# Two PSUM banks in the attention: one per kind of product, or both for every kind in turn

## The chip, the cores and the metric

The kernel runs on one core of one Trainium2 chip. The metric is the time of one execution on the device in microseconds (us). Matrix products run on TensorE (PE in the profile; its weight loads are PEld), elementwise work on VectorE (DVE), ScalarE (ACT) and GpSimd (POOL), and DMAs are issued by SyncE (SP).

## The reference

One block over 1024 tokens of width 1024: a normalized input is projected, an mLSTM branch and a differential attention branch are computed from the projections, both are gated, mixed, projected out and added to the input. The change lies in the attention branch (8 heads, values of width 128, two maps of queries and keys of width 64 in each head):

```python
def diff_attention(q, k, v, lam):
    ...
    def one_block(qb):
        scores = jnp.einsum('bqhjd,bkhjd->bhjqk', qb, k) * scale
        p = jax.nn.softmax(scores, axis=-1)
        p_diff = p[:, :, 0] - lam * p[:, :, 1]
        return jnp.einsum('bhqk,bkhd->bqhd', p_diff, v)
    ...
att = rmsnorm(att, da_subln_g[layer]) * (1.0 - lambda_init)
y_b = att.reshape(B, S, DA_WIDTH).astype(x.dtype) * jax.nn.silu(b_z)
```

## The kernel before, in words

The kernel has stages that follow each other on TensorE: the projections of the mLSTM branch, then the attention, then the mLSTM, then the products behind both branches. Every float32 matrix is split into a high and a low part, so a product is three matmuls.

In the attention a head has eight blocks of 128 queries. For block t of head h these units are recorded:

- S(h,t), `scores` (L924): 12 matmuls into two PSUM tiles of two banks each. VectorE takes the maximum of each (L927), ScalarE the exponential of each (L929), and VectorE joins both maps into one (L935).
- T(h,t,0) and T(h,t,1), `transposes` (L131 in the helper `tr`): four transpositions each into a bank with the tag T. ScalarE casts them to the high part pH (L948), then VectorE subtracts to get the low part pL (L949). Only then is the bank free.
- PV(h,t2,0) and PV(h,t2,1), `pv` (L960): the products with v for two blocks, 24 matmuls into one bank with the tag PV, which ScalarE copies to att (L962).
- M(h,t2), `squares` (L131): two transpositions of att into a bank with the tag PV, which ScalarE squares and sums in place (L972).
- G(h,0) and G(h,1), `scale` (L131): four transpositions into a bank T, read by VectorE (L992).

PSUM has eight banks: four for S, one T, one PV, and two (tag pj) for the projections that are woven in as filler. The filler is the projections of the next head (q and k with the rotary embedding in `da_proj`, v in `da_v`, z) and gate projections; L429 and L451 are their matmuls. Rotated q and k are cast and split (L863 to L869), written to memory by SP as stk (L873) and read back in another layout as qq and kst (L875) before the scores of the next head use them.

The order on TensorE is written by a planner, `Weaver`. It keeps a clock in its own units: each unit has a cost, the units it comes after, and, for a bank, a time `hold` for which the bank stays taken once the unit is done. At every step it takes the list (attention or filler) whose first unit is ready earliest:

```python
        if u.tag:
            held = sorted(self.free.get(u.tag, []))
            n = self.banks.get(u.tag, 1)
            if len(held) >= n:
                t = max(t, held[-n])
```

So a tag that is not named in `banks` counts as one bank. The planner's counts are its own; how many banks a tag really has is set by `banks("ps1", ...)`, and a real bank is handed out in rotation. TensorE keeps the planned order; the order on the other engines is set by the framework's scheduler from the recorded program.

## Time and profile before

| | |
|---|---|
| median of 3 runs | 1750.76 us (1749.43 to 1751.54) |
| profiled execution | 1750.27 us |
| its span | 1748.5 us |
| mean granted TensorE clock | 0.992 |
| attention with its filler | about 440 to 1155 us of the span |

The profile is of one execution. A busy TensorE row is pipelined, so matmuls overlap in it. In the rows of the prediction a group stands as line, engine, operation, output tile <- input tiles; in rows in order of time the first number is the start and the second the duration, both in us, and a bracket at the end gives idle time of that engine before the instruction and who ended it.

### The profile page before, as it was taken

The page shows a single profiled execution, that of the slowest core. Times are in us where ns is not written, and L with a number is a line of the kernel's source. Part 1 is how long each engine was busy: PE and PEld are TensorE (multiplying, and loading weights), DVE is VectorE, ACT ScalarE, POOL GpSimd, SP SyncE. Part 2 cuts the span into 40 slices and gives each one's busy share as a digit, 9 for nine tenths or more (in the row PEclk, how much of TensorE's full clock was granted, in tenths as well). Part 3 has the DMA queues.
Part 4 walks back from the last instruction along what each step waited for, and adds up shares of the span by engine and source line. Part 5 has one row for each costly group of instructions (what it writes and reads, how often), then busy time and mean ns, then how long its engine had stood idle before and what let it go on. Part 6 is the DMA issues. An engine that isn't in the chain of part 4 may idle for free. (4 is left out here: it accounts for less than half of the span.)

```text
span 1748.5 us, 25290 instructions
## 1 busy us (share of the span) xinstructions
PE 1664.4 (95%) x9431; PEld 1390.5 (80%) x9431; DVE 990.8 (57%) x1799; ACT 780.6 (45%) x1554; POOL 608.6 (35%) x680
## 2 busy tenths in 40 slices
PE   7999999999999999999999989999999989999998
PEld 5777887877877877787778767789999877888887
DVE  5777678772476665666656655414666753226533
ACT  7454555552354544454445444424555643112211
POOL 4767666664142323323341322132312311222000
PEclk9999999999999999999999999999999999999999
DMA  5343434434241214230422041146545327444222
GB/s 179 92 136 110 145 109 133 138 116 150 79 128 62 89 37 133 73 91 24 139 75 82 27 130 61 43 146 192 149 143 150 105 77 255 145 126 150 85 85 84
DMA packets 182540, 195.55 MB, mean 112 GB/s; under 512 B 10905, under 2 KB 134130, under 8 KB 182418
## 3 DMA queue, kind: packets, MB, share of 16 engines
q1 hardware_dynamic: 181506, 192.35, 35.4%
q8 instruction: 74, 1.21, 0.3%
q10 hardware_dynamic: 912, 1.59, 0.2%
q14 instruction: 48, 0.39, 0.1%
HBM read 130.89 MB, written 63.01 MB: 111 GB/s over the span
## 5 line engine op out<-in xcount | busy, mean ns | idle before, releaser
L429 PE MATMUL pj<-hH,wH 128*128 128x512 f32 x640 | 267.3, 418 | 3.8 <-DVE hl L864 1.9
L429 PE MATMUL pj<-hH,wL 128*128 128x512 f32 x640 | 252.3, 394 | 1.8 <-POOL wL L207 1.8
L429 PE MATMUL pj<-hL,wH 128*128 128x512 f32 x640 | 251.4, 393 | 0.2 <-DVE hL L580 0.2
L209 POOL TENSOR_TENSOR wL<-raw,wH 128x1024 fp32r<-128x1024 f32 x41 | 99.5, 2426 | 273.2 <-ACT wH L204 264.9
L929 ACT ACTIVATE e<-S,nm 128x1024 f32<-128x1024 f32 x128 | 142.6, 1115 | 106.6 <-DVE nm L927 106.3
L949 DVE TENSOR_TENSOR pL<-T,pH 128x512 fp32r<-128x512 f32 x128 | 88.2, 689 | 136.7 <-ACT pH L948 136.6
L927 DVE TENSOR_REDUCE nm<-S 128x1 f32<-128x1024 f32 x128 | 150.6, 1218 | 25.5 <-PE S L924 24.8
L429 PEld LDWEIGHTS pj<-hH,wH 128*128 128x128 f32 x640 | 121.0, 189 | 40.4 <-issue 17.2
L451 PE MATMUL pj<-wH,hH 128*128 128x256 f32 x512 | 150.2, 293 | 0.8 <-DVE zg L882 0.5
L451 PE MATMUL pj<-wL,hH 128*128 128x256 f32 x512 | 144.9, 283 | 1.4 <-POOL wL L207 1.4
L429 PEld LDWEIGHTS pj<-hH,wL 128*128 128x128 f32 x640 | 120.9, 189 | 30.4 <-POOL wL L207 3.2
L451 PE MATMUL pj<-wH,hL 128*128 128x256 f32 x512 | 144.6, 282 | 0.0
L429 PEld LDWEIGHTS pj<-hL,wH 128*128 128x128 f32 x640 | 121.4, 190 | 19.2 <-DVE hL L580 0.6
L429 PE MATMUL pj<-sl_yb,wH 128*128 128x512 f32 x384 | 120.7, 394 | 4.6 <-ACT sl_yb L1315 2.2
L131 PE MATMUL T<-ident,e 128*128 128x128 f32 x512 | 78.8, 277 | 36.9 <-DVE pL L949 36.7
L924 PE MATMUL S<-kst,qq 64*128 64x512 f32 x768 | 111.3, 422 | 0.7 <-ACT e L929 0.5
L948 ACT CAST pH<-T 128x512 fp32r<-128x512 f32 x128 | 74.9, 585 | 80.8 <-PE T L131 80.4
L204 ACT CAST wH<-raw 128x1024 fp32r<-128x1024 f32 x56 | 58.8, 1050 | 113.4 <-PE pj L429 96.4
L131 PEld LDWEIGHTS T<-ident,e 128*128 128x128 f32 x512 | 60.4, 141 | 58.2 <-DVE pL L949 49.0
L451 PEld LDWEIGHTS pj<-wH,hH 128*128 128x128 f32 x512 | 97.8, 191 | 6.1 <-issue 4.3
L451 PEld LDWEIGHTS pj<-wL,hH 128*128 128x128 f32 x512 | 97.6, 191 | 2.3 <-POOL wL L207 2.3
L451 PEld LDWEIGHTS pj<-wH,hL 128*128 128x128 f32 x512 | 97.8, 191 | 0.2
(358 smaller groups left out, 4117.1 us busy)
## 6 DMA issues: line engine op xcount, KB each, us to landing
raw<-in_w_in_dram SPq DMA_DIRECT2D x88, 512.0 KB
stk<-hl SPq DMA_DIRECT2D x64, 256.0 KB
qq<-stk SPq DMA_DIRECT2D x16, 512.0 KB
kst<-stk SPq DMA_DIRECT2D x16, 512.0 KB
x<-in_x_dram SPq DMA_DIRECT2D x8, 512.0 KB
cak<-y SPq DMA_DIRECT2D x16, 256.0 KB
cakH<-cin SPq DMA_DIRECT2D x16, 256.0 KB
cakL<-tz SPq DMA_DIRECT2D x16, 256.0 KB
```

Of the source, the lines that this page charges most:

```text
L131: self.t.transpose(out, in_, self.ident[0:k, 0:k])
L204: self.a.copy(wH, raw)
L209: self.p.tensor_tensor(out=wL, in0=raw, in1=wHf, op=ALU.subtract)
L429: self.t.matmul(ps, lhsT=l[:, k, :], rhs=r, start=(n == 0), stop=(n == 23))
L451: self.t.matmul(ps[:, i, :], lhsT=l, rhs=r[:, k, :], start=(kh == 0 and k == 0 and m == 0), stop=(kh == 1 and k == 3 and m == 2))
L924: self.t.matmul(ps[:, o], lhsT=qq[r, x, c], rhs=k[r, y, o], start=(m == 0), stop=(m == 2))
L927: v.tensor_reduce(out=nm, in_=ps, axis=AX.X, op=ALU.max, negate=True)
L929: a.activation(out=e, in_=ps, func=AF.Exp, bias=nm[:, 0:1], accum_out=Z[:, j, t:t + 1])
L948: a.copy(pH[:, :, s], ps)
L949: v.tensor_tensor(out=pL[:, :, s], in0=ps, in1=pH[:, :, s].bitcast(F32), op=ALU.subtract)
```

## The change

The bank of tag PV is given to tag T: `pv` and `squares` take their bank with the tag T, the pool has two T banks and no PV bank, and the planner is told of two T banks. Four banks for S and two for the projections stay.

```diff
         def pv(t2, g):
             vH, vL = st["v"]
             if g == 0:
-                st["pv"] = self.bank("PV")
+                st["pv"] = self.bank("T")
...
         def squares(t2):
-            pt = self.bank("PV")
+            pt = self.bank("T")
...
-            PV=lambda t2, g: Unit(12 * TP, lambda: pv(t2, g), tag="PV" if g == 0 else None, hold=LAG["PVh"], name=("PV", h, t2, g),
+            PV=lambda t2, g: Unit(12 * TP, lambda: pv(t2, g), tag="T" if g == 0 else None, hold=LAG["PVh"], name=("PV", h, t2, g),
...
-            M=lambda t2: Unit(2 * TP, lambda: squares(t2), tag="PV", hold=LAG["Mh"], name=("M", h, t2),
+            M=lambda t2: Unit(2 * TP, lambda: squares(t2), tag="T", hold=LAG["Mh"], name=("M", h, t2),
...
-            w.add(leave("ps0", "s0", "tf"), enter("w1", "w1", side="right"), banks("ps1", S=2, T=1, PV=1))
-            w.banks.update(S=1)
+            w.add(leave("ps0", "s0", "tf"), enter("w1", "w1", side="right"), banks("ps1", S=2, T=2))
+            w.banks.update(S=1, T=2)
```

The planner then writes another order of the units inside the attention; before and behind it TensorE's order is the same. TensorE in the cycle of S(2,2), before (S is the scores, pj a filler matmul, PV<-ident,att is M, T<-ident,e is T(2,1,0)):

```order
L924 MATMUL S<-kst,qq 128x512 x12
L429 MATMUL pj<-hH_170,wH 128x512
L429 MATMUL pj<-hL_172,wH 128x512
L429 MATMUL pj<-hH_170,wL 128x512
L131 MATMUL PV<-ident,att 128x128 x2
L429 MATMUL pj<-hH_170,wH 128x512
L429 MATMUL pj<-hL_172,wH 128x512
L429 MATMUL pj<-hH_170,wL 128x512
L131 MATMUL T<-ident,e_5724 128x128 x4
```

The same place now (M is T<-ident,att):

```order
L924 MATMUL S<-kst,qq 128x512 x12
L429 MATMUL pj<-hH_170,wH 128x512
L429 MATMUL pj<-hL_172,wH 128x512
L429 MATMUL pj<-hH_170,wL 128x512
L429 MATMUL pj<-hH_170,wH 128x512
L429 MATMUL pj<-hL_172,wH 128x512
L429 MATMUL pj<-hH_170,wL 128x512
L429 MATMUL pj<-hH_170,wH 128x512
L429 MATMUL pj<-hL_172,wH 128x512
L429 MATMUL pj<-hH_170,wL 128x512
L131 MATMUL T<-ident,att 128x128 x2
L131 MATMUL T<-ident,e_5724 128x128 x4
```

Nine filler matmuls stand ahead of M where three stood, and none between M and the first T; twelve follow that T before the second T in both.

ScalarE at the same place, before (L972 is M's two squares, L929 the exponentials of S(2,2), L948 the casts of the two T):

```order
L972 ACTIVATE PV_5848,ms_4747<-PV_5848 128x128
L929 ACTIVATE e0_5835,Z_5624<-S_5819,nm_5833 128x1024
L972 ACTIVATE PV_5848,ms_4747<-PV_5848 128x128
L929 ACTIVATE e1_5839,Z_5624<-S_5820,nm_5837 128x1024
L948 CAST pH_5779<-T_5872 128x4x128
L948 CAST pH_5810<-T_5895 128x4x128
```

And now:

```order
L929 ACTIVATE e0_5822,Z_5624<-S_5806,nm_5820 128x1024
L929 ACTIVATE e1_5826,Z_5624<-S_5807,nm_5824 128x1024
L972 ACTIVATE T_5848,ms_4747<-T_5848 128x128
L948 CAST pH_5779<-T_5869 128x4x128
L972 ACTIVATE T_5848,ms_4747<-T_5848 128x128
L948 CAST pH_5791<-T_5888 128x4x128
```

The two squares have moved behind both exponentials, and the cast of the first T stands between them.

ScalarE ahead of the exponentials of S(2,6), before (L868 casts the rotated q and k of the next head, L193 casts a weight):

```order
L948 CAST pH_6185<-T_6187 128x4x128
L193 CAST wH_6214<-raw_5801 128x8x64
L193 CAST wH_6214<-raw_6093 128x8x64
L868 CAST hl_6198<-m0_6078 128x512
L948 CAST pH_6232<-T_6234 128x4x128
L868 CAST hl_6198<-m1_6079 128x512
L972 ACTIVATE PV_6270,ms_5625<-PV_6270 128x128
L929 ACTIVATE e0_6257,Z_5624<-S_6241,nm_6255 128x1024
```

And now:

```order
L948 CAST pH_6185<-T_6187 128x4x128
L193 CAST wH_6223<-raw_5836 128x8x64
L193 CAST wH_6223<-raw_6093 128x8x64
L948 CAST pH_6214<-T_6216 128x4x128
L868 CAST hl_6198<-m0_6085 128x512
L868 CAST hl_6198<-m1_6086 128x512
L929 ACTIVATE e0_6251,Z_5624<-S_6235,nm_6249 128x1024
L929 ACTIVATE e1_6255,Z_5624<-S_6236,nm_6253 128x1024
```

The second T's cast now stands ahead of both casts L868, and these stand together right ahead of the exponentials.

## The prediction

> **What bounds the kernel now.** I read the page's first part, then the busy time of the three stages, then who waited for whom on TensorE inside the attention, and then single cycles in order of time. The page says that TensorE is the engine that counts:

> ```profile
> span 1748.5 us, 25290 instructions
> PE 1664.4 (95%) x9431; PEld 1390.5 (80%) x9431; DVE 990.8 (57%) x1799; ACT 780.6 (45%) x1554; POOL 608.6 (35%) x680
> ```

> TensorE idles 1748.5 - 1664.4 = 84 us in all. The attention with its filler runs from about 440 to 1155 us; its row (length; busy us of PE, PEld, DVE, ACT, POOL; granted clock), and TensorE's longest waits there (us in total, times, longest):

> ```profile
> 440.00:1155.00 715.00, 677.33 (x4204) 556.89 (x4203) 411.11 (x564) 329.81 (x677) 211.56 (x200) 0.99 0.26 79
> ```
> ```profile
> PE T L131 <- DVE pL L949: 36.7, 27, 2.8
> PE S L924 <- ACT e L929: 0.5, 1, 0.5
> ```

> Of 37.7 idle us, 36.7 are 27 waits of one kind: a transposition T cannot start because VectorE has not read the T before it out of the only T bank. VectorE (411 of 715 us) and ScalarE (330) have room, so this is latency, not load. One such wait, the cycle of head 2 with the scores S(2,2): TensorE, then ScalarE, then VectorE.

> ```profile
> 631.62 1.67 PE L924 MATMUL S<-kst,qq 64*128 64x512 f32 x12
> 634.03 0.38 PE L131 MATMUL PV<-ident,att 128*128 128x128 f32 x2
> 634.95 0.60 PE L131 MATMUL T<-ident,e 128*128 128x128 f32 x4
> ...
> 637.68 0.39 PE L429 MATMUL pj<-hL,wH 128*128 128x512 f32 x1
> 637.91 0.39 PE L429 MATMUL pj<-hH,wL 128*128 128x512 f32 x1
> 639.83 0.66 PE L131 MATMUL T<-ident,e 128*128 128x128 f32 x4 [1.53 <-DVE pL L949]
> ```
> ```profile
> 635.87 0.28 ACT L972 ACTIVATE PV<-PV 128x128 f32<-128x128 f32 x1
> 636.06 0.19 ACT L972 ACTIVATION_READ_ACCUMULATOR PV<-PV 128x1 f32 x1
> 636.15 1.11 ACT L929 ACTIVATE e<-S,nm 128x1024 f32<-128x1024 f32 x1
> 637.15 0.20 ACT L929 ACTIVATION_READ_ACCUMULATOR e<-S,nm 128x1 f32 x1
> 637.24 0.59 ACT L948 CAST pH<-T 128x512 fp32r<-128x512 f32 x1
> ```
> ```profile
> 633.33 2.36 DVE L927 TENSOR_REDUCE nm<-S 128x1 f32<-128x1024 f32 x2 [0.23 <-PE S L924]
> 637.89 1.29 DVE L935 SCALAR_TENSOR_TENSOR e<-e,r,e 128x1024 f32<-128x1024 f32 x1
> 639.09 0.69 DVE L949 TENSOR_TENSOR pL<-T,pH 128x512 fp32r<-128x512 f32 x1
> ```

> The first T of the cycle starts at 634.95; its cast stands behind both exponentials (637.24) and its subtraction behind VectorE's L935 (639.09 to 639.78). The second T could have started at 639.83 - 1.53 = 638.30 and starts at 639.83. So a T bank can be held 4.8 us, and the filler between two T covers 3.4.

> The waits have a second price. The granted clock stood at 0.50 in four stretches of this stage, each at the end of a wait or just behind it (one of these waits is shown):

> ```profile
> 526.12:529.53 3.41, 3.41 (x14) 2.35 (x11) 2.18 (x3) 0.41 (x2) 0.00 (x0) 0.50 0.27 96
> 683.14:689.96 6.82, 6.18 (x21) 4.22 (x22) 2.77 (x4) 0.59 (x1) 1.28 (x1) 0.50 0.45 138
> 898.18:901.59 3.41, 3.41 (x14) 2.29 (x15) 1.27 (x2) 0.00 (x0) 1.49 (x1) 0.50 0.26 103
> 1027.88:1031.29 3.41, 3.41 (x14) 2.25 (x14) 0.69 (x1) 0.59 (x1) 1.28 (x1) 0.50 0.26 102
> ```
> ```profile
> 896.75 0.66 PE L131 MATMUL T<-ident,e 128*128 128x128 f32 x4 [1.79 <-DVE pL L949]
> ```

> At half clock half of a stretch is lost: 1.7 us for each of 3.41, 3.4 for that of 6.82.

> [...]

> **The change, part by part.** Instructions and their durations stay. Two things move: which bank a group waits for, and, because the planner now counts two banks of one kind, where the filler stands.

> *T behind T.* Now the second T of a cycle no longer waits for the first, but for the group two before it. All 36.7 us have that old cause, so all go, if the new owner of the bank is out in time.

> *T behind a product.* In the cycles with a product PV the second T waits for the copy L962. From the rows of one:

> ```profile
> 564.78 0.28 PE L960 MATMUL PV<-pH,vL 128*128 128x256 f32 x1
> ```
> ```profile
> 565.10 0.37 ACT L962 COPY att<-PV 128x256 f32<-128x256 f32 x1 [2.12 <-PE PV L960]
> ```

> The bank is free 565.47 - 564.78 = 0.7 us after the last product matmul starts; the new order puts a T and 3 or more filler matmuls in between. Cost nothing; the cover is ScalarE's idle time before that copy (2.12 us), and if that is gone, the second T is late.

> *T behind M* (the transposition of att whose squares are L972). In the cycle above the new order has 21 filler matmuls between S and the second T where 18 stood, at 0.23 each (637.91 - 637.68): the T comes at 638.30 - 631.62 + 0.69 = S + 7.37, and M, with nine matmuls ahead of it where three stood, at 634.03 - 631.62 + 1.38 = S + 3.79. Its bank is M's, and ScalarE's new order is exponential, exponential, square, cast of the first T, square. The first exponential can start after one reduction, 633.33 + 1.2 = S + 2.9; each takes 1.2; squares 0.38 each, the cast 0.59: free at S + 2.9 + 2.4 + 0.38 + 0.59 + 0.38 = S + 6.7. Slack 0.7, against a wait of 1.53 before. Where two casts L868 (0.62 each, row below) now stand ahead of the exponentials and hold them up for their full time, the bank is 1.24 - 0.67 = 0.57 late. The new order has this at S(h,2) and S(h,4) of heads 1, 3, 5 and S(h,4) of heads 2, 4, 6: nine sites, 9 x 0.57 = 5 us lost. The bounds are 0 (squares before the cast, as at some places) and 9 x 1.24 = 11.

> *What is late next.* Keys of the next head go through memory (stk, then kst). The second half of kst is already just in time for head 5. The rows of heads 3, 5 and 7: the reader of the last projection (L863), the issue of that load, the scores (of head 5 their second half), and TensorE's waits between (3.9 us stand both in 671.3:699.5 and in 842.5:868.2, 5.4 in 1013.2:1041.6):

> ```profile
> 676.97 0.62 ACT L868 CAST hl<-m 128x512 fp32r<-128x512 f32 x1
> ```
> ```profile
> 671.96 0.68 DVE L863 TENSOR_TENSOR hl<-pj,sinT 128x512 f32<-128x512 f32 x1
> 843.20 0.68 DVE L863 TENSOR_TENSOR hl<-pj,sinT 128x512 f32<-128x512 f32 x1
> 1013.91 0.68 DVE L863 TENSOR_TENSOR hl<-pj,sinT 128x512 f32<-128x512 f32 x1
> ```
> ```profile
> 693.76 0.46 SPq L875 DMA_DIRECT2D kst<-stk  x1
> 863.22 0.46 SPq L875 DMA_DIRECT2D kst<-stk  x1
> 1033.04 0.46 SPq L875 DMA_DIRECT2D kst<-stk  x1
> ```
> ```profile
> 698.42 1.66 PE L924 MATMUL S<-kst,qq 64*128 64x512 f32 x12
> 868.16 0.96 PE L924 MATMUL S<-kst,qq 64*128 64x512 f32 x6 [0.29 <-DMA kst<-stk]
> 1040.68 1.67 PE L924 MATMUL S<-kst,qq 64*128 64x512 f32 x12
> ```
> ```profile
> PE T L131 <- DVE pL L949: 3.9, 3, 2.8
> PE T L131 <- DVE pL L949: 5.4, 3, 2.8
> ```

> In head 5 TensorE waited for the load, so it is usable 868.16 - 863.22 = 4.94 after its issue, 24.96 after L863. Its second half is needed six matmuls, 0.96 us, after S starts. With 4.94 for all three, TensorE cannot gain more before heads 3, 5, 7 than 699.38 - 698.70 = 0.7, 0 and 1041.64 - 1037.98 = 3.7 us, though 3.9, 3.9 and 5.4 of waits stand there: SP and POOL take this path in the same order in both programs. A wait for kst of some 2 us there may bring a half-clock stretch: I charge one, 1.7. Net 4.4 - 1.7 = 2.7. Heads 2, 4 and 6 have their keys ready earlier: no wait for kst stands there now.

> *The sum.* Waits outside these three stretches 36.7 - 3.9 - 3.9 - 5.4 = 23.5; half clock outside them (526, 898) 3.4; inside 2.7; lost at M's bank 5: gain 24.6. The profiled execution took 1750.27 us (span 1748.5), 0.5 below the median of the runs; 1750.27 - 24.6 gives 1726 us. Behind the attention nothing is reordered, and TensorE is busy there too, so the gain is kept to the end.

> **Rivals.** (1) *Partly eaten*: half of the 23.5 comes back at M's bank, the stretches before heads 3, 5 and 7 gain nothing, and the half clock stays as it is: 11.8 won, 1738 us. For it: ScalarE can be later than I walked. In head 2 the squares of an M ended 680.21 - 676.15 = 4.1 us after it, over the 3.6 that I count on (7.37 - 3.79):

> ```profile
> 676.15 0.38 PE L131 MATMUL PV<-ident,att 128*128 128x128 f32 x2
> ```
> ```profile
> 680.02 0.19 ACT L972 ACTIVATION_READ_ACCUMULATOR PV<-PV 128x1 f32 x1
> ```

> (2) *Slower*: M's bank becomes the wait of every head. Its second square stands behind two exponentials and a cast in ScalarE's queue, and 32 M each hold up a T. At 0.77 us each the 24.6 are gone; at 1.2 each the time is 1726 + 38 = 1764. Against it: that needs M's bank held 4.8 us as a rule, and the one above, with two L868 ahead, was held 4.1. [...] (3) *No change*: the waits turn into waits of S for exponentials, since the two score banks are as tight; 1750. Against it: that wait was 0.5 us once. (4) *More*: kst lands earlier as well and nothing is lost at M: 23.5 + 3.4 + 9, near 1714; the floor, all waits and all half clock gone, is 1750.27 - 36.7 - 8.5 = 1705.

> **Chances.** The forecast (1715 to 1735) 0.62, partly eaten 0.20, slower 0.09, no change 0.04, more 0.05. A measurement tells 0.2% (3.5 us) from no change. Faster 0.62 + 0.20 + 0.05 = 0.87, same 0.04, slower 0.09. The range reaches from near the fourth rival to past the first: 1714 to 1744.

> **What would show it.** After the change the wait of T for pL should be near 0; in its place short waits of T for the second square, under 6 us in all, and waits of S for kst before heads 3, 5, 7, 1 to 3 us each. The attention stage should be about 690 us long, with at most two stretches of half clock. Wrong would be: over 10 us of waits for the squares, waits for pL that stay because VectorE's order is late, or a stage behind the attention that grows by what this one saves.

## The result and the profile after

The changed kernel took 1721.24 us (median, 1718.37 to 1722.36) against 1750.93 us before: a ratio of 0.9829, 95% interval 0.9812 to 0.9846. The forecast was 1726. The profiled execution took 1722.36 us, 27.9 less than the profiled one of before; the sum had said 24.6.

The page's first part, after:

```profile
span 1720.5 us, 25270 instructions
PE 1660.1 (96%) x9431; PEld 1392.5 (81%) x9431; DVE 988.8 (57%) x1799; ACT 777.5 (45%) x1554; POOL 605.6 (35%) x680
```

Span minus busy TensorE is now 60.4 us, where it was 84. The stretch that holds the same 4204 matmuls as 440 to 1155 did, and TensorE's waits in it:

```profile
440.65:1125.80 685.15, 671.26 (x4204) 557.51 (x4203) 408.89 (x564) 326.82 (x677) 208.77 (x200) 0.99 0.26 83
```
```profile
PE S L924 <- DMA kst<-stk: 8.0, 3, 2.7
PE T L131 <- ACT T L972: 5.6, 6, 1.4
PE T L131 <- DVE pL L949: 0.3, 1, 0.3
```

The stage is 685.15 long where it was 715.00: 29.85 us went here, and some 2 came back outside it. Idle fell from 37.7 to 13.9 us, and the wait that filled it, T for pL, from 36.7 to 0.3. What is left are the two waits that the prediction named: S for the next keys, and T for M's squares. Note the second number of the long row too: TensorE's *busy* time for the same instructions fell by 6.1 us (677.33 to 671.26). No wait shows that part; some 1.7 us of it are half clock, by the estimate below.

One cycle shows how the second bank works, and where it fails. TensorE in the cycle of S(2,6), after:

```profile
660.71 1.66 PE L924 MATMUL S<-kst,qq 64*128 64x512 f32 x12
664.47 0.38 PE L131 MATMUL T<-ident,att 128*128 128x128 f32 x2
664.69 0.60 PE L131 MATMUL T<-ident,e 128*128 128x128 f32 x4
669.16 0.66 PE L131 MATMUL T<-ident,e 128*128 128x128 f32 x4 [1.12 <-ACT T L972]
```

M (664.47) and the first T (664.69) are issued back to back into two banks; with one bank each they could do that before as well. What is new is that the second T (669.16) waits for M's bank and no longer for the first T's. ScalarE says why M's bank is late here:

```profile
664.01 0.62 ACT L868 CAST hl<-m 128x512 fp32r<-128x512 f32 x1 [2.88 <-POOL m L865]
665.25 0.62 ACT L868 CAST hl<-m 128x512 fp32r<-128x512 f32 x1 [0.62 <-POOL m L866]
665.77 1.11 ACT L929 ACTIVATE e<-S,nm 128x1024 f32<-128x1024 f32 x1
667.97 0.27 ACT L972 ACTIVATE T<-T 128x128 f32<-128x128 f32 x1
668.25 0.58 ACT L948 CAST pH<-T 128x512 fp32r<-128x512 f32 x1
668.91 0.19 ACT L972 ACTIVATION_READ_ACCUMULATOR T<-T 128x1 f32 x1
```

The casts L868 themselves wait for GpSimd (the brackets). The second runs until 665.87, the exponentials start behind it, and the second square ends at 669.10, just before the T can start. This is the place whose new order on ScalarE was shown with the change. Six places of this sort have the wait: 0.64 us in heads 1, 3 and 5, and 1.1 to 1.4 in heads 2, 4 and 6.

### The profile page after: what moved, and what is told of

It reads as the page before. It is cut to its first block, busy times and chain, and to the rows that moved or that the text cites. A ratio compares the mean times of both kernels' runs of the same rounds, so it can differ in the third digit from the quotient of the medians.

```text
span 1720.5 us, 25270 instructions
## 1 busy us (share of the span) xinstructions
PE 1660.1 (96%) x9431; PEld 1392.5 (81%) x9431; DVE 988.8 (57%) x1799; ACT 777.5 (45%) x1554; POOL 605.6 (35%) x680
## 5 line engine op out<-in xcount | busy, mean ns | idle before, releaser
L429 PE MATMUL pj<-hH,wH 128*128 128x512 f32 x640 | 269.1, 420 | 3.8 <-DVE hl L864 1.9
L429 PE MATMUL pj<-hH,wL 128*128 128x512 f32 x640 | 253.7, 396 | 1.8 <-POOL wL L207 1.8
L429 PE MATMUL pj<-hL,wH 128*128 128x512 f32 x640 | 253.0, 395 | 0.2 <-DVE hL L580 0.2
L929 ACT ACTIVATE e<-S,nm 128x1024 f32<-128x1024 f32 x128 | 142.5, 1115 | 104.7 <-DVE nm L927 104.6
L927 DVE TENSOR_REDUCE nm<-S 128x1 f32<-128x1024 f32 x128 | 150.4, 1217 | 16.7 <-PE S L924 15.9
L429 PEld LDWEIGHTS pj<-hH,wH 128*128 128x128 f32 x640 | 122.2, 191 | 39.2 <-issue 15.4
L949 DVE TENSOR_TENSOR pL<-T,pH 128x512 fp32r<-128x512 f32 x128 | 87.9, 688 | 108.7 <-ACT pH L948 107.8
L429 PEld LDWEIGHTS pj<-hH,wL 128*128 128x128 f32 x640 | 121.9, 190 | 30.8 <-POOL wL L207 3.3
L429 PEld LDWEIGHTS pj<-hL,wH 128*128 128x128 f32 x640 | 122.6, 192 | 18.7 <-DVE hL L580 0.6
L429 PE MATMUL pj<-sl_yb,wH 128*128 128x512 f32 x384 | 121.8, 397 | 4.3 <-ACT sl_yb L1315 2.4
L924 PE MATMUL S<-kst,qq 64*128 64x512 f32 x768 | 108.8, 413 | 8.0 <-DMA kst<-stk 8.0
L948 ACT CAST pH<-T 128x512 fp32r<-128x512 f32 x128 | 74.9, 585 | 88.0 <-PE T L131 87.5
L924 PEld LDWEIGHTS S<-kst,qq 64*128 64x128 f32 x768 | 68.3, 186 | 35.4 <-issue 10.5
L429 PEld LDWEIGHTS pj<-sl_yb,wH 128*128 128x128 f32 x384 | 73.4, 191 | 22.3 <-DVE sl_yb L1316 3.4
```

Source lines behind the costliest of these rows:

```text
L429: self.t.matmul(ps, lhsT=l[:, k, :], rhs=r, start=(n == 0), stop=(n == 23))
L924: self.t.matmul(ps[:, o], lhsT=qq[r, x, c], rhs=k[r, y, o], start=(m == 0), stop=(m == 2))
L927: v.tensor_reduce(out=nm, in_=ps, axis=AX.X, op=ALU.max, negate=True)
L929: a.activation(out=e, in_=ps, func=AF.Exp, bias=nm[:, 0:1], accum_out=Z[:, j, t:t + 1])
L948: a.copy(pH[:, :, s], ps)
L949: v.tensor_tensor(out=pL[:, :, s], in0=ps, in1=pH[:, :, s].bitcast(F32), op=ALU.subtract)
```

## The experiments

Each kernel was timed in three rounds beside the kernel before on the same chip; ratios are to that kernel.

**The banks without the new order.** The kernel before with two shared banks; the planner keeps its old tags and counts, so TensorE keeps the order of before.

```diff
-                st["pv"] = self.bank("PV")
+                st["pv"] = self.bank("T")
...
-            pt = self.bank("PV")
+            pt = self.bank("T")
...
-            w.add(leave("ps0", "s0", "tf"), enter("w1", "w1", side="right"), banks("ps1", S=2, T=1, PV=1))
+            w.add(leave("ps0", "s0", "tf"), enter("w1", "w1", side="right"), banks("ps1", S=2, T=2))
```

> The two banks of after, handed to T, PV and M in turn, with TensorE's order of before (the planner still counts one T and one PV bank). Theory A, the real second bank is what frees TensorE: the 27 waits of T for pL (36.7 us) go here too; what is left is T behind M's squares (6 to 10 us) and the wait for kst before heads 3, 5, 7 (about 8 us), 1720 to 1728 us. Theory B, the planner's new places for the filler bring the larger part (its own clock shows 13 us less): 1737 to 1745 us, with over 15 us of waits of T left.

Measured: 1722.19 us, ratio 0.9842 (0.9828 to 0.9857). TensorE's waits in the attention, banks alone:

```profile
PE S L924 <- DMA kst<-stk: 8.9, 2, 5.3
PE T L131 <- DVE pL L949: 2.6, 3, 1.9
PE T L131 <- ACT att L962: 1.2, 1, 1.2
```

The whole effect is there with the old order, within what the intervals tell. The waits for M's squares, of which 6 to 10 us were expected here, are not there: M stands early in that order. In their place are short waits for pL and for the copy of att, and longer ones for kst.

**The order without the banks.** The changed kernel's order of units, with one bank T and one bank PV.

```diff
-                st["pv"] = self.bank("T")
+                st["pv"] = self.bank("PV")
...
-            pt = self.bank("T")
+            pt = self.bank("PV")
...
-            w.add(leave("ps0", "s0", "tf"), enter("w1", "w1", side="right"), banks("ps1", S=2, T=2))
+            w.add(leave("ps0", "s0", "tf"), enter("w1", "w1", side="right"), banks("ps1", S=2, T=1, PV=1))
```

> TensorE's order of after (the planner counts two T banks) with the banks of before, one for T and one for PV and M. Theory A: in this order the two T of the odd blocks stand 1 us apart where the bank is held 2.0 to 2.1 at least, so about 28 waits of 1 us come on top of the old ones at the even blocks: 50 to 70 us of waits for pL, 1760 to 1790 us. Theory B, the order is worth 13 us by itself: 1737 us or less.

Measured: 1770.48 us, ratio 1.0120 (1.0105 to 1.0136), slower. Its longest entry in the list of waits:

```profile
PE T L131 <- DVE pL L949: 48.7, 50, 3.6
```

That is just under the 50 to 70 us expected. The new order leans on the second bank and costs without it. Together the two runs settle what the gain came from: the second bank behind T, not the planner's new places.

**The needed load first.** The changed kernel, with the load of kst issued ahead of that of qq in each half.

```diff
-            for i, x in enumerate((qq, st["k"][:, :, c])):
+            for i, x in ((1, st["k"][:, :, c]), (0, qq)):
```

> After, but SP issues the load of kst ahead of that of qq (in after qq goes first). The three waits for kst (2.6 to 2.7 us before heads 3, 5, 7, 8.0 in all) are the part of the gain that the prediction capped. Theory A, the path from the last projection to kst sets the start of these heads: kst is usable 0.4 to 1.5 us earlier, the waits fall to 3.5 to 7 us, 1717 to 1721 us. Rival, all bytes of both loads land together and their order counts for nothing: 8 us as before and the time of after.

Measured: 1713.23 us, ratio 0.9793 (0.9776 to 0.9809): better than expected. TensorE's waits in the attention, kst first:

```profile
PE T L131 <- ACT T L972: 5.6, 6, 1.4
PE S L924 <- DMA kst<-stk: 2.8, 3, 1.3
```

Of 8.0 us of waits for kst 5.2 went; 2.8 is less than the 3.5 to 7 that were expected. The rest of the gain is clock: the three stretches at half clock behind these waits (below) went too, worth another 6.8. From the first S to the last M the stage is 10.8 us shorter than in the changed kernel, against 5.2 + 6.8 = 12.0.

**The keys used later.** The changed kernel, with the planner told that the next head's keys take 20 of its units instead of 14 from their projection to S; it puts more filler ahead of S(h,0).

```diff
-LAG = dict(Th=2.2, Sh=5.0, PVh=3.7, Mh=8.1, qk=14.0, ...
+LAG = dict(Th=2.2, Sh=5.0, PVh=3.7, Mh=8.1, qk=20.0, ...
```

> After, with the planner's delay from the last projection of q and k to the scores raised from 14 to 20: four filler units (2.8 us) move ahead of the first scores of heads 3, 5 and 7, nothing else but the places behind. Theory A, these waits are idle time that filler can fill and they bring the three half-clock stretches of after (684, 851, 1015): the wait for kst falls from 8.0 to under 1 us, most of the half clock there (6.8 us lost) goes, 1708 to 1716 us. Rival, the loss only moves: the filler is missing between the T behind these scores, which then wait for M's squares 1.5 to 2 us each: 1717 to 1722 us.

Measured: 1707.79 us, ratio 0.9762 (0.9748 to 0.9777), just below the 1708 to 1716 that were expected. The first scores of head 3, which are broken by a wait in the changed kernel, come in one piece:

```profile
683.30 1.89 PE L924 MATMUL S<-kst,qq 64*128 64x512 f32 x12
```

No wait for kst and no stretch at half clock are left in the attention. 8.0 + 6.8 = 14.8 us of the changed kernel's time hung on these three loads, and 14.5 of them came off between the first S and the last M.

**A planner that follows the rotation.** The changed kernel's planner may take either bank once one is free, while the real banks come in turn (all but behind a G, as shown further below). Here it counts in turn, and M's hold is cut to 4.8.

```diff
-            held = sorted(self.free.get(u.tag, []))
+            held = self.free.get(u.tag, [])
...
-LAG = dict(Th=2.2, Sh=5.0, PVh=3.7, Mh=8.1, qk=14.0, ...
+LAG = dict(Th=2.2, Sh=5.0, PVh=3.7, Mh=4.8, qk=14.0, ...
```

> After, with a planner that counts banks as the pool hands them out (the bank taken n groups before, not the one that is free first) and holds M's bank 4.8 instead of 8.1. Theory A: the 5.6 us of waits of T for M's squares come from T standing 7.4 us behind S where the bank is free later; the new plan puts about 2 us more filler there, so they go, 5.6 to under 1 us; the waits for kst stay at about 8 or grow by what was waited for just ahead of them (3.7), to 8 to 12: 1717 to 1723 us. Rival: the filler is now missing elsewhere and as much comes back in waits of T for pL.

Measured: 1724.39 us, ratio 0.9856 (0.9838 to 0.9874): no gain, where 1717 to 1723 us were expected. Its waits in the attention:

```profile
PE S L924 <- DMA kst<-stk: 13.4, 3, 5.0
PE T L131 <- ACT att L962: 2.6, 1, 2.6
```

All waits for M's squares are gone, 5.6 us, but TensorE only reaches the keys sooner: 5.4 us more of waits there, and longer half-clock stretches, 3.41 us once and 6.83 three times, where the changed kernel had 6.83 once and 3.41 twice. The 3.41 lies behind the new wait of 2.6 us for the copy of att. The expectation allowed 8 to 12 us of waits for kst and left out the clock. While the keys are the last thing to end before heads 3, 5 and 7, time won ahead of them is given back there with interest.

**Both edits of the keys' path.** kst first and qk=20 in one kernel.

> After with both edits on the keys' path, kst ahead of qq and the delay of 20. Theory A: with the delay alone no wait for kst is left, so the order of the loads has nothing more to give: the same time as the delay alone within 2 us, with 5.6 us of waits for M's squares. Rival: the loads compete with others, and their order is worth the 8 us that it gave alone: 1697 to 1702 us.

Measured: 1706.60 us, ratio 0.9753 (0.9735 to 0.9771). It has the lowest median here, but the edit of the loads adds nothing measurable to the later use of the keys: once S no longer waits for kst, an earlier kst buys nothing here (1706.60 against 1707.79 us). The attention's waits that are left:

```profile
PE T L131 <- ACT T L972: 5.6, 6, 1.4
PE T L131 <- DVE pL L949: 0.4, 1, 0.4
```

**The casts on GpSimd.** The kernel just named, with the casts L868, the suspects for M's late bank, moved from ScalarE to GpSimd.

```diff
-                a.copy(hl[:, i, :], m[i])
+                p.tensor_copy(hl[:, i, :], m[i])
```

> As both edits, and the two casts L868 of the rotated q and k run on GpSimd instead of ScalarE. Theory A, these casts stand in ScalarE's queue ahead of the exponentials and so keep M's bank: the six waits of T for the squares (5.6 us) go to under 1 us. GpSimd's path to the keys gets some 2.6 us longer, which the delay of 20 may not cover in full: up to 3 us of waits for kst. Against both edits 2 to 5 us less. Rival, M's bank is held by the squares and the cast between them alone: the six waits stay at 4 us or more.

Measured: 1707.61 us, ratio 0.9758 (0.9737 to 0.9779): no gain, where 2 to 5 us were expected. TensorE's waits from 200 us to the end of the attention, casts on GpSimd, then the same row of the kernel before this edit:

```profile
PE pj L429 <- DVE hl L864: 4.1, 1, 4.1
PE S L924 <- DMA kst<-stk: 3.3, 3, 1.2
...
PE T L131 <- ACT T L972: 0.6, 1, 0.6
```
```profile
PE pj L429 <- DVE hl L864: 1.9, 1, 1.9
```

The cause of the wait for the squares is shown: without these casts on ScalarE 5.0 of its 5.6 us are gone. The time isn't won, because the path of q and k got longer on GpSimd: waits for kst come back, 3.3 us, and one wait ahead of the attention grows by 2.2 us. From the first S to the last M the kernel is 2.5 us shorter. But its first S comes 2.4 us later (459.8 against 457.4), and behind the last M it takes 1.7 us longer, with two more windows at half clock there. Which of GpSimd's instructions are late at that place was not followed.

**The keys' path, before the change.** kst first and qk=20 in the kernel before.

> Before (one T bank, one PV bank) with both edits on the keys' path. Theory A, before the change the keys were not late, since the waits of T stood ahead of the scores: the wait for kst (0.3 us) goes, nothing else, within 3 us of before. Rival, the keys' path cost time by itself: 5 us or more less than before.

Measured: 1751.29 us, ratio 1.0012 (0.9997 to 1.0027).

```profile
PE T L131 <- DVE pL L949: 38.6, 30, 2.8
```

The edit that is worth some 13 us behind the change (0.9829 to 0.9753) is worth nothing ahead of it: the T bank set the pace, and the keys came in time.

## Why the prediction was right, and where it was off

**T for pL, 36.7 us: right.** 0.3 us is left, and the banks alone do it.

**M's bank: the mechanism was right, the size too large.** Nine sites at 0.57, 5 us, were charged; outside the stretches before heads 3, 5 and 7 there were three, 1.9 us in all, one of which is (heads 3 and 5 have the same):

```profile
548.11 0.66 PE L131 MATMUL T<-ident,e 128*128 128x128 f32 x4 [0.64 <-ACT T L972]
```

These three are S(h,2) of heads 1, 3 and 5, where 0.57 was near. The step that failed is the six sites at S(h,4): the prediction took the cycle S(2,2), in which the second T comes 7.37 us after S, for all nine. At S(2,4) both casts L868 do stand ahead of the exponentials, but the second T comes much later. TensorE (the scores, the first and the second T), then ScalarE:

```profile
639.71 1.66 PE L924 MATMUL S<-kst,qq 64*128 64x512 f32 x12
646.91 0.60 PE L131 MATMUL T<-ident,e 128*128 128x128 f32 x4
650.12 0.60 PE L131 MATMUL T<-ident,e 128*128 128x128 f32 x4
```
```profile
644.27 1.11 ACT L929 ACTIVATE e<-S,nm 128x1024 f32<-128x1024 f32 x1
645.38 0.27 ACT L972 ACTIVATE T<-T 128x128 f32<-128x128 f32 x1
645.66 1.11 ACT L929 ACTIVATE e<-S,nm 128x1024 f32<-128x1024 f32 x1
646.75 0.27 ACT L972 ACTIVATE T<-T 128x128 f32<-128x128 f32 x1
```

The second square, with the 0.38 that it takes with its sum, ends at 646.75 + 0.38 = 647.13, S + 7.4. At S + 7.37 a T would just have met it; the second T comes at 650.12 - 639.71 = 10.41, S + 10.4, since G and twelve more filler matmuls stand between M and the first T. The first T (646.91) starts before the second square is over, so it has G's bank and not M's: behind a G the two banks do not strictly alternate, and M's bank goes to the second T here too. ScalarE's other order, one square ahead of the second exponential, makes little difference: from the first exponential to the end of the second square 647.13 - 644.27 = 2.9 us pass, and 669.10 - 665.77 = 3.3 in the cycle of S(2,6) above. The three other waits, 1.1 to 1.4 us at S(h,6) of heads 2, 4 and 6, lie right ahead of S(3,0), S(5,0) and S(7,0), where TensorE would have waited for the keys in any case. They are longer than 0.57 because the casts had to wait for GpSimd: at S(2,6) the exponentials start 665.77 - 660.71 = 5.1 us after S, where the prediction had 2.9 + 1.24.

**The stretches before heads 3, 5 and 7: too small a gain.** The prediction held the chain from L863 to S fixed. After the change its rows are these (VectorE, SyncE, TensorE):

```profile
660.24 0.68 DVE L863 TENSOR_TENSOR hl<-pj,sinT 128x512 f32<-128x512 f32 x1
826.18 0.68 DVE L863 TENSOR_TENSOR hl<-pj,sinT 128x512 f32<-128x512 f32 x1
990.77 0.68 DVE L863 TENSOR_TENSOR hl<-pj,sinT 128x512 f32<-128x512 f32 x1
```
```profile
679.78 0.61 SPq L875 DMA_DIRECT2D kst<-stk  x1
845.56 0.77 SPq L875 DMA_DIRECT2D kst<-stk  x1
1009.87 1.32 SPq L875 DMA_DIRECT2D kst<-stk  x1
```
```profile
684.47 1.65 PE L924 MATMUL S<-kst,qq 64*128 64x512 f32 x6 [2.74 <-DMA kst<-stk]
850.32 0.96 PE L924 MATMUL S<-kst,qq 64*128 64x512 f32 x6 [2.64 <-DMA kst<-stk]
1015.16 1.22 PE L924 MATMUL S<-kst,qq 64*128 64x512 f32 x4 [2.59 <-DMA kst<-stk]
```

Each wait was inside the 1 to 3 us that were named. But from L863 to the half of S that waits, 24.2, 24.1 and 24.4 us now pass (684.47 - 660.24, and so on) where 27.4, 24.96 and 27.7 did: 3.2, 0.8 and 3.3 won, 7.3 in all, and 4.4 had been counted. The load is usable 4.7, 4.8 and 5.3 us after its issue, so the 4.94 held. The step that failed is that the issue stayed where it was behind L863: in head 3 it came 21.8 us after (693.76 - 671.96) and comes 19.5 after now (679.78 - 660.24). In head 5 it moved from 20.0 to 19.4, in head 7 not at all (19.1), and there 3.3 of the 3.7 counted came. In head 3 SyncE was done issuing the four stores of stk 8.1 us after L863 before the change and 8.5 after it (676.37 + 3.64 = 680.01 and 664.66 + 4.04 = 668.70), and the load of qq, which waits for them and goes ahead of that of kst, followed 13.3 and 10.7 us later (693.34 and 679.36). So it is the wait for the stores that got shorter; why was not followed.

**Half clock: charged once, came three times.** The two stretches outside went, as said. Behind each of the three waits for kst there is one now, three where the prediction allowed two at most:

```profile
684.05:690.88 6.83, 6.41 (x18) 4.62 (x19) 3.32 (x5) 2.56 (x5) 0.00 (x0) 0.50 0.29 77
851.30:854.71 3.41, 3.41 (x8) 2.67 (x9) 2.36 (x2) 2.13 (x3) 0.00 (x0) 0.50 0.47 139
1015.14:1018.55 3.41, 3.39 (x10) 2.32 (x11) 1.71 (x2) 0.45 (x1) 0.00 (x0) 0.50 0.57 154
```

13.65 us at half clock, 6.8 lost, where 17.07 us lost 8.5 before: of the 3.4 won outside, half is left. That half of a stretch is lost is an estimate from the 0.50 of its row, here as in the prediction; by the starts of the filler matmuls it is a little less: in the stretch from 851.30 they stand (853.89 - 851.75) / 5 = 0.43 us apart, at full clock 0.23, so about 46% is lost, 6.3 and 7.9 us. Of the old loss 5.1 lay between L863 and S, where the keys set the end; the new stretches lie behind S and count in full.

**What makes up the 29.85.** Waits outside the three stretches 23.5 - 1.9 - 0.3 = +21.3; those stretches +7.3; half clock outside them, two new ones of 3.41 behind S(5,0) and S(7,0) and one of 6.83 behind S(3,0) for the old two, 3.4 - 6.8 = -3.4 (half of their length each). That makes 25.2, so 4.6 us remain, in which TensorE is recorded as busy. This is about 0.24 us for each of the 19 waits that are gone (29 before, with one of 0.3 for kst, and 10 after), and the rows have a place for it. In the prediction's cycle the matmul at 637.91 had a neighbour 0.23 later as a rule, so the T could have started at 638.14, but the idle time counts from the end of its row, 638.30: 0.16 us of the wait is not recorded as one. And the group of four T behind a wait lasts 0.66 where one without lasts 0.60.

All ten traces bear it out. The table has TensorE's waits in the stage, and its busy time there for the same number of matmuls, less half of what fell into stretches at half clock:

| kernel | waits | busy, us |
|---|---|---|
| order without the banks | 52 | 674.6 |
| keys' path, before the change | 31 | 669.2 |
| before | 29 | 669.0 |
| kst first | 11 | 665.2 |
| after | 10 | 664.5 |
| keys later | 8 | 664.3 |
| both edits of the keys' path | 8 | 664.0 |
| banks without the order | 7 | 664.2 |
| casts on GpSimd | 5 | 663.7 |
| planner that follows the rotation | 5 | 662.6 |

A line through them rises by 0.24 us a wait and misses none by more than 0.9. The first two rows and the eighth tell that it goes with the waits and not with the order.

**How near the sum came.** 24.6 was forecast and 27.9 measured, and that is partly luck. Against the sum, M's bank gave 3.1 us more, the three stretches 2.9 and the unrecorded part of the waits 4.6, of which the sum had nothing; the clock gave 5.1 less, the work beyond the attention 1.9 and the wait left for pL 0.3. Misses of 10.6 one way and 7.3 the other leave 3.3.

**Beyond the attention.** The work around it kept the gain but for some 2 us: a stretch at half clock ahead of the stage is new (3.41 us from 428.05), and one behind it is 6.83 us long from 1452.05, where it was 3.41. The first need not come from the change: of the ten traces seven have it, the keys' path before the change among them, and three do not. Of the rivals, *partly eaten* counted on M's bank and fell with it; *no change* needed S to wait for exponentials, and no such wait is left; *slower* needed M's bank held 4.8 us as a rule, and it was held longer than its cover at six sites only; *more*, at 1714, had the keys earlier and nothing lost at M: part of both came, and 1721 lies between it and the forecast.

## What to carry to other kernels

When a buffer is the wait and another with the same life stands beside it, let both kinds of work use both, but check on the reader's engine when the *other* kind lets go: here, with the banks in turn, late readers of M held up T six times, 5.6 us in all. Before you count the gain, look up what the next consumer waits for: the keys' path was worth nothing before this change and some 13 us after it. Each of the three waits for kst, 2.59 to 2.74 us, cost its length and, by the estimate of half, another 1.7 or 3.4 us in the stretch of 3.41 or 6.83 us at a clock of 0.50 behind it, so take the longest waits first.

## What was not expected of the hardware

**When the half clock comes.** In each of the two traces, before and after, the stretches in the attention begin on one grid of 3.413 us: the starts of before, 526.12, 683.14, 898.18 and 1027.88, lie 46, 63 and 38 steps apart (501.76 us in 147 steps), and those of after, 684.05, 851.30 and 1015.14, lie 49 and 48 apart (331.09 us in 97). So I divided the attention into such windows, in before, after and four of the experiments (the banks without the order, the order without the banks, the planner that follows the rotation, the keys' path before the change). In every one of the 21 windows at full clock in which TensorE idled 1.89 us or more (length minus the first busy number), the next window ran at half; in none where it idled 1.79 or less; between them it went both ways (1.80 us half, 1.86 not). Three windows of after, then two of before with the window behind the first of them; the clock is the third number from the end:

```profile
680.64:684.05 3.41, 1.09 (x8) 0.48 (x6) 1.75 (x3) 1.66 (x3) 2.35 (x1) 1.00 0.85 303
847.89:851.30 3.41, 0.98 (x7) 0.57 (x7) 1.20 (x2) 0.36 (x1) 1.81 (x1) 1.00 0.61 208
1011.73:1015.14 3.41, 0.84 (x6) 0.35 (x6) 1.49 (x3) 1.40 (x3) 2.35 (x1) 1.00 0.70 247
```
```profile
553.43:556.84 3.41, 1.62 (x10) 1.08 (x10) 2.88 (x6) 1.95 (x4) 2.98 (x6) 1.00 0.26 84
556.84:560.26 3.42, 3.42 (x22) 2.29 (x21) 2.27 (x4) 0.59 (x1) 2.44 (x2) 1.00 0.26 98
894.77:898.18 3.41, 1.61 (x10) 1.03 (x11) 3.20 (x5) 1.63 (x2) 3.00 (x7) 1.00 0.25 86
```

**A wait cost more than its idle time**, by about 0.24 us here, as the table of the ten traces shows.
